# Where the operand sums of one weight pair are made, and when one stage asks for its factors, in an fp32 encoder block

## The chip, the cores and the metric

The kernel runs on one core of a Trainium2 chip, with five engines that work side by side: PE (TensorE, matrix products), DVE (VectorE), ACT (ScalarE), POOL (GpSimd) and SP (SyncE, which here only issues DMAs). Each engine takes its instructions in program order and waits on semaphores for the others. The metric is the device time of one execution in microseconds (us); three runs of the kernel before were timed, and one more was profiled.

## The reference, cut to what matters

One layer over 1024 tokens of width 1024, all in fp32. `w_in` holds the columns of all the projections side by side.

```python
h = rmsnorm(x, norm_g)
q, k, v, za, u, vs, zs, gm = split(h @ w_in)
a = window_sink_attention(rope(q), rope(k), v, sinks)
a = (a * silu(za)) @ w_att_out
sgo = chunked_spatial_gating(gelu(u), gelu(vs), ...)     # 128x128 mixing per channel group
sgo = (sgo * silu(zs)) @ w_sg_out
ga, gs = split(sigmoid(gm + b_merge))
y = ga * a + gs * sgo
out = rmsnorm(x + y @ w_o, final_g)
```

The change lies in the projections zs (its silu multiplies the gated branch) and gs (one of the two merge gates).

## The kernel before, in words

**Products.** The weights are packed as 82 tiles `w[i]` of 128 x 1024. All large products but that of `vs` are made by a Strassen-Winograd scheme on pairs of weight tiles (`gemm_pair`, L364 for the matmuls): a pair has four quarters of 128 x 512, a11 and a12 (the halves of its first tile) and a21 and a22 (of its second), and takes seven products in place of eight. Their left sides are a11, a12, a22 and four sums of quarters: s1 = a21 + a22, s2 = s1 + a11, s3 = a11 + a21, and s4 = a12 + s2, with the signs folded elsewhere. Each product is 12 matmuls: every operand is split into a rounded part (`wh`, an ACT cast, L154) and a rest (`wl`, a DVE subtraction, L155), and high x high, high x low and low x high are added in PSUM over four slices. In time the seven products run in the order 0, 2, 3, 1, 4, 5, 6; products 2 and 3 need the tile with s1 and s2, products 4 and 5 the one with s3 and s4.

**Two ways to the sums.** A pair made with `pair_job` loads its quarters (four DMAs of 256 KB, tiles `wr`) and DVE adds them (`sums`, L251 to L255: four instructions into two `s` tiles). For a pair made with `early_job` the sums are made in DRAM long before, by six DMAs of the POOL queue, some of them with an adding write (L310, tile `sums`); the pair then loads a11 and a12 as one DMA, a22 as another, and the two tiles of sums (`s<-sums`, 2 x 512 KB). These six steps of all such pairs, with 16 steps for `w_o`, stand in a list `early`, sorted so that step 0 of a first group of eight pairs comes first, then step 1 of all eight, and so on, and then the rest. `part_of_early` takes one from the list: in the `vs` stage at every second call and at every call of its fifth tile (`1 if t == 4 else 2`), in the u pairs at each product, and again in the locked stage below. Each waits for the latest `pace` instruction of a product.

**Order of the pairs.** u (4 pairs), kv (1), q (4), zs (2 of its 4), then the locked stage with gs (4) and ga (4), then zs (2), za, and the output projections. A pair's job begins (its loads are issued, and its splits enter a list) when one split of the pair before is left (`split_next`). `make_sums` gives DVE its additions: in a pair of the zs stage right behind the split for product 6 of the pair that runs.

**The zs stage (`zs_pair`).** For each of its four output tiles ACT takes silu (L1079), DVE multiplies by a factor that an earlier stage left in DRAM (L1088), and the product goes to DRAM (L495). The first zs pair loads its factors as two DMAs of 512 KB into `qhl` tiles, which the q stage used until then; the second loads four of 256 KB into `rot` tiles. The program's names for these DRAM tensors drop the digits, so the factors appear as `qhl<-s_dr` and `rot<-s_dr`, all at L201, the helper that issues on SP's queue. Between the zs products `hook()` runs what is left of the q stage: the first query tiles (`q<-q_hl`) and the last rotation.

**The locked stage.** Each of its eight pairs (`locked_pair`) interleaves the seven products with attention for four steps; PE, ACT and DVE follow an order written by hand here. The scores of a step (L1135) go to two PSUM banks `ps_sc`. For the step, DVE takes maxima (L1160) and ACT exponentials (L1170), and only then are the banks free for the next step's scores. In the first locked pair the scores of step 0 stand ahead of product 0, and those of step 1 in the middle of product 2. Banks `ps_o` are two as well: product 2 of a pair takes the one in which product 5 of the pair before ended, once DVE has read that (L406, which ends the pair's third output tile).

Elsewhere the scheduler of the program chooses the order on each engine, from the program's order and its own estimates.

Of the kernel before, what the change touches and what calls it, by code (L numbers as in the profile page):

```python
# [25 lines left out]
F32 = mybir.dt.float32  # L26
# [5 lines left out]
P = 128  # L32
D = 1024
S = 1024
KC = D // P
HALF = 512
# [11 lines left out]
W_SG = 58  # L48
# [5 lines left out]
def hybrid_tile(  # L54
# [25 lines left out]
    def nm(s):  # L80
        count[0] += 1
        return f"{s}_{count[0]}"
# [4 lines left out]
    def mtile(shape, dt, tag, bufs, pool=None):  # L87
        return (pool or main).tile(shape, dt, name=nm(tag), tag=tag, bufs=bufs)

    def scratch(name, shape=(D, S)):  # L90
        return dram.tile(list(shape), F32, name=name)
# [29 lines left out]
    s1_dr = scratch("s1_dr")  # L121
# [78 lines left out]
    def copy_to(dst, src):  # L200
        nc.sync.dma_start(dst, src)  # L201
# [38 lines left out]
    def half_of(half):  # L240
        return slice(half * HALF, (half + 1) * HALF)
# [26 lines left out]
    def pair_job(n, load):  # L268


        def job():
            r0, r1 = raw_tile(), raw_tile()
            for j in range(2):
                load(r0[:, half_of(j)], 0, j)
            for j in range(2):
                load(r1[:, half_of(j)], 1, j)
            sa, sb = sums(r0[:, 0:HALF], r0[:, HALF:D], r1[:, 0:HALF], r1[:, HALF:D])
            return [
                (r0[:], [(n, 0), (n, 1)]),
                (sa, [(n, 2), (n, 3)]),  # L280
                (sb, [(n, 4), (n, 5)]),
                (r1[:, HALF:D], [(n, 6)]),
            ]

        return job
# [5 lines left out]
    early = []  # L291
# [12 lines left out]
    def early_job(n, i0, i1):  # L304

        made = dram.tile([P, 4, HALF], F32, name=f"sums_{n}")
        s1, s3, s2, s4 = (made[:, i, :] for i in range(4))

        def step(dst, src, op=ALU.bypass):
            return lambda: paced(nc.gpsimd.dma_start(dst, src, accum_op=op))  # L310

        early.append(
            (
                step(made[:, 0:2, :], w[i1][:, 0:HALF].unsqueeze(1).broadcast_to([P, 2, HALF])),
                step(made[:, 2:4, :].rearrange("p a n -> p (a n)"), w[i0]),
                step(s1, w[i1][:, HALF:D], ALU.add),
                step(s3, w[i0][:, 0:HALF], ALU.add),
                step(s2, s1, ALU.add),
                step(s4, s2, ALU.add),
            )  # L320
        )

        def job():
            r0, r1 = raw_tile(), raw_tile()
            copy_to(r0[:], w[i0])
            copy_to(r1[:, HALF:D], w[i1][:, HALF:D])
            loaded = []

            def load_sums():
                for a in range(2):  # L330
                    v = mtile([P, D], F32, "s", 2)
                    copy_to(
                        v[:].rearrange("p (b n) -> p b n", b=2),
                        made[:].rearrange("p (b a) n -> p a b n", a=2)[:, a],
                    )
                    loaded.append(v)

            sums_to_load.append(load_sums)
            if not locked[0]:
                load_made()  # L340
            return [
                (r0[:], [(n, 0), (n, 1)]),
                (lambda: loaded[0][:], [(n, 2), (n, 3)]),
                (lambda: loaded[1][:], [(n, 4), (n, 5)]),
                (r1[:, HALF:D], [(n, 6)]),
            ]

        return job
# [66 lines left out]
    def of_w(i0, i1):  # L415
        return lambda dst, i, j: copy_to(dst, w[(i0, i1)[i]][:, half_of(j)])

    def of_token_w(base, m):


        def load(dst, i, j):
            first, c0 = base + 4 * ((m + i) // 4) + 2 * j, ((m + i) % 4) * P
            d = dst.rearrange("p (c k n) -> p c k n", c=2, k=2)
            for c in range(2):
                copy_to(d[:, c], w[first + c].rearrange("p (k n) -> p k n", k=2)[:, :, c0 : c0 + P])

        return load
# [8 lines left out]
    def add_pairs(base, step, pairs, made=False):  # L436
        for m in pairs:
            i0, i1 = base + step * m, base + step * (m + 1)
            if made:
                jobs.append(early_job(len(jobs), i0, i1))  # L440
            else:
                load = of_w(i0, i1) if step else of_token_w(base, m)
                jobs.append(pair_job(len(jobs), load))

    ALL = range(0, KC, 2)
# [1 line left out]
    jobs.append(pair_job(len(jobs), of_kv))  # L447
    add_pairs(W_Q, 0, ALL)
    add_pairs(W_ZS, 1, (0, 2))
    add_pairs(W_SG, 2, ALL, True)  # L450
    add_pairs(W_ATT, 2, ALL, True)
    add_pairs(W_ZS, 1, (4,), True)
    add_pairs(W_ZS, 1, (6,))
# [3 lines left out]
        add_pairs(base, 2, (4, 6))  # L457
    N_PAIRS = len(jobs)
    written[0] = N_PAIRS
    early = [steps[i] for some in (early[:KC], early[KC:]) for i in range(6) for steps in some]  # L460


    def o_quarter(j, half):
# [22 lines left out]
    def part_of_early(every=2):  # L486
        hooks[0] += 1
        if early and hooks[0] % every == 0:
            early.pop(0)()
# [4 lines left out]
    def put(dst, m, half, src, queue=nc.sync):  # L494
        queue.dma_start(place(dst, m, half), src)  # L495

    def get(src, m, half, bufs, tag="g"):
        g = mtile([P, HALF], F32, tag, bufs, pool)
        copy_to(g[:], place(src, m, half))
        return g  # L500
# [99 lines left out]
    def vs_step(acc, t, k, wh, wl):  # L600

        hi, lo = (v[:, k % 4, :] for v in quarter_of(t, k // 4))
        for n, (lt, rt) in enumerate(((hi, wh), (hi, wl), (lo, wh))):
            mm = nc.tensor.matmul(acc, lt, rt, start=k == 0 and n == 0, stop=k == KC - 1 and n == 2)  # L604
        return mm
# [47 lines left out]
    def vs_weights(c):  # L653
        raw = raw_tile()
        nc.sync.dma_start(raw[:], w[W_VS + 4 + c])
        hi = mtile([P, D], F32R, "wh", 3)
        lo = mtile([P, D], F32R, "wl", 3)
        split(hi[:], lo[:], raw[:])
        return hi, lo
# [55 lines left out]
    for c in range(4):  # L715
        if c + 2 < 4:
            weights.append(vs_weights(c + 2))
        for t in range(NT):
            wh, wl = weights[c]
            for k in range(2):  # L720
                ks = half_of(k)
                pace[0] = vs_step(accs[t][:], t, 2 * c + k, wh[:, ks], wl[:, ks])
            part_of_early(1 if t == 4 else 2)
            if c == 3:
                nc.scalar.activation(xh[:, t, HALF:D], accs[t][:], AF.Gelu)
            if aside and t % 2:
                aside.pop(0)()
# [18 lines left out]
    pool = stage.enter_context(tc.tile_pool(name="mixing", bufs=1))  # L746
    late = []

    def hook():
        for _ in range(2):  # L750
            if late:
                late.pop(0)()
# [84 lines left out]
    pool = stage.enter_context(tc.tile_pool(name="keys", bufs=1))  # L837
# [44 lines left out]
    pool = stage.enter_context(tc.tile_pool(name="queries", bufs=1))  # L882
# [141 lines left out]
    steps = [(g, t, par) for g in range(2) for t in range(NT) for par in range(2)]  # L1024
# [47 lines left out]
    gates = []  # L1072
    last_silu = [None]

    def zs_pair(m, hook):
        silus, hooked = [], [0]

        def finish(i, half, q, src, sign):
            last_silu[0] = nc.scalar.activation(q[:], src, AF.Silu, scale=sign)  # L1079
            silus.append((i, half, q))  # L1080

        def step():
            hook()
            hooked[0] += 1
            if hooked[0] >= 4:
                while silus:
                    i, half, q = silus.pop(0)
                    nc.vector.tensor_mul(q[:], q[:], gates.pop(0))  # L1088
                    put(s_dr, m + i, half, q[:])

        if m:
            gates.extend(get(s1_dr, m + i, half, 5, "rot")[:] for i, half in ((0, 0), (1, 1), (0, 1), (1, 0)))
        else:
            rows = [mtile([P, 2, HALF], F32, "qhl", 3, pool) for _ in range(2)]
            for i in range(2):
                copy_to(rows[i][:].rearrange("p h n -> p (h n)"), s1_dr[i * P : (i + 1) * P, :])
            gates.extend(rows[i][:, half, :] for i, half in ((0, 0), (1, 1), (0, 1), (1, 0)))
        gemm_pair(hb, finish, step)

    steps_of_q += [first_loads(), rotate(1, 1)]  # L1100
    zs_pair(0, part_of_q)
    zs_pair(2, part_of_q)
    after(nc.scalar.activation(warm[:], eps_sb[:], AF.Exp), last_silu[0])
    stage.close()
# [3 lines left out]
    pool = stage.enter_context(tc.tile_pool(name="attention", bufs=1))  # L1108
# [304 lines left out]
    with tc.manual_schedule(engines={mybir.EngineType.PE, mybir.EngineType.Activation, mybir.EngineType.DVE}):  # L1413
        p = 0
# [27 lines left out]
    pool = stage.enter_context(tc.tile_pool(name="later", bufs=1))  # L1442
# [248 lines left out]
    rows = [load_rows(p) for p in range(3)]  # L1691
# [9 lines left out]
    for p in range(4):  # L1701
        n, t, acc, x11 = N_PAIRS + p, T_ORDER[p], accs[p], firsts[p]
# [173 lines left out]
```

## Time and profile before

| | us |
|---|---|
| three runs | 935.73, 934.78, 933.14 (median 934.78) |
| profiled execution | 935.56 |
| its span, first to last instruction | 933.8 |
| PE busy | 910.1 |
| DVE busy | 690.6 |
| ACT busy | 530.3 |
| POOL busy | 147.0 |

The span is what the rows of the trace lie in; 1.8 us of the profiled time lie around it. A row of the timeline has the start in us from the span's start, the duration, engine and line, the operation with output and inputs, and in brackets how long the engine had stood idle before it and what ended that. In a row of the windows stand PE, PEld (weight load), DVE, ACT and POOL busy time, then the clock granted to PE (1 is full), the mean busy share of the 16 DMA engines and GB/s.

### The profile page before, as it was taken

What the parts mean: (1) busy time and instruction counts of PE and PEld (TensorE: products, weight loads), DVE (VectorE), ACT (ScalarE), POOL (GpSimd) and SP (SyncE); (2) the same over time, 40 slices, a digit from 0 to 9 for tenths busy, and PEclk for the clock granted to TensorE, in tenths of its full rate; (3) what the DMA queues carried; (4) which work ended last, traced back from release to release, by engine and by line L of the source; (5) the groups of instructions that cost most, each with busy time, mean ns of one, the idle gap of its engine ahead of it and who ended that gap; (6) DMA issues with size and microseconds to landing.
All of it is one profiled execution on the core that took longest, in us unless ns stands there. A gap on an engine that the chain in (4) does not pass through costs nothing.

```text
span 933.8 us, 13145 instructions
## 1 busy us (share of the span) xinstructions
PE 910.1 (97%) x4285; PEld 752.5 (81%) x4285; DVE 690.6 (74%) x1230; ACT 530.3 (57%) x1054; POOL 147.0 (16%) x215
## 2 busy tenths in 40 slices
PE   7999999999999989999999999999999999999996
PEld 5788888888888768888888887888887887888885
DVE  5784686665677747778887788666699689669986
ACT  6873433333444546777777778443475565458443
POOL 1002322213011002212221111101110011210012
PEclk9999999999999999999999999999999999999999
DMA  7239988877788879999999897775558654999623
GB/s 251 99 113 232 222 155 182 176 162 219 239 273 261 257 248 302 249 263 248 252 328 263 237 273 201 266 239 179 180 199 315 211 197 157 294 295 302 208 108 118
DMA packets 129708, 209.50 MB, mean 224 GB/s; under 512 B 12680, under 2 KB 59272, under 8 KB 129640
## 3 DMA queue, kind: packets, MB, share of 16 engines
q1 hardware_dynamic: 107256, 147.58, 49.4%
q0 software_dynamic: 22240, 60.83, 27.3%
q8 instruction: 34, 0.56, 0.2%
q14 instruction: 34, 0.28, 0.1%
q10 hardware_dynamic: 144, 0.26, 0.1%
HBM read 151.87 MB, written 92.41 MB: 262 GB/s over the span
## 4 chain that ended last, share of the span: by engine, by line
PE 39%; DVE 13%; ACT 7%; issue 3%; DMA 1%; ACTq 0%; DVEq 0%
PE ps_mm L364 19%; PE ps_o L364 11%; PE ps_tp L364 3%; ACT pr L1170 2%; PE ps_sc L364 2%; DVE sm L1160 2%; DVE aT L1273 1%; DVE pTb L1242 1%; ACT pr L1193 1%; PE ps_sc L1135 1%; PE ps_o L1259 1%; DVE wl L155 1%; DVE bq L184 1%; ACT aT L1272 1%; DVE pT L1234 1%
## 5 line engine op out<-in xcount | busy, mean ns | idle before, releaser
L154 ACT CAST wh<-s 128x1024 fp32r<-128x1024 f32 (+1 forms) x78 | 78.0, 1002 | 86.1 <-PE ps_mm L364 39.8
L155 DVE TENSOR_TENSOR wl<-s,wh 128x1024 fp32r<-128x1024 f32 (+1 forms) x78 | 91.4, 1172 | 26.0 <-ACT wh L154 25.8
L155 DVE TENSOR_TENSOR wl<-wr,wh 128x1024 fp32r<-128x1024 f32 (+1 forms) x64 | 60.4, 947 | 58.1 <-ACT wh L154 57.8
L154 ACT CAST wh<-wr 128x1024 fp32r<-128x1024 f32 (+1 forms) x64 | 52.9, 829 | 78.0 <-PE ps_mm L364 38.0
L310 POOL DMA_DIRECT2D sums<-in_w_dram x52 | 39.0, 903 | 218.7 <-PE ps_mm L604 64.3
L1170 ACT ACTIVATE pr<-ps_sc,sm 128x192 f32<-128x192 f32 (+2 forms) x128 | 51.2, 407 | 32.7 <-DVE sm L1161 24.6
L364 PE MATMUL ps_o<-T_b22h,wh 128*128 128x512 f32 x148 | 59.3, 401 | 0.0
L364 PE MATMUL ps_o<-T_t1h,wh 128*128 128x512 f32 x148 | 59.1, 399 | 0.3 <-ACT wh L154 0.2
L364 PE MATMUL ps_o<-T_t1h,wl 128*128 128x512 f32 x148 | 58.3, 394 | 0.0
L364 PE MATMUL ps_o<-T_t1l,wh 128*128 128x512 f32 x148 | 58.1, 393 | 0.0
L364 PE MATMUL ps_o<-T_b22h,wl 128*128 128x512 f32 x148 | 57.8, 390 | 0.0
L364 PE MATMUL ps_o<-T_b22l,wh 128*128 128x512 f32 x148 | 57.8, 390 | 0.0
L364 PE MATMUL ps_mm<-T_b11h,wl 128*128 128x512 f32 x140 | 54.8, 392 | 2.1 <-DVE wl L155 2.1
L364 PE MATMUL ps_mm<-T_t2h,wh 128*128 128x512 f32 x140 | 55.5, 396 | 0.8 <-ACT x L385 0.8
L364 PE MATMUL ps_mm<-T_b11h,wh 128*128 128x512 f32 x140 | 55.1, 393 | 0.0
L364 PE MATMUL ps_mm<-T_t4h,wh 128*128 128x512 f32 x140 | 54.9, 392 | 0.0
L364 PE MATMUL ps_mm<-T_t3h,wh 128*128 128x512 f32 x140 | 54.8, 391 | 0.0
L364 PE MATMUL ps_mm<-T_b11l,wh 128*128 128x512 f32 x140 | 54.7, 391 | 0.0
L364 PE MATMUL ps_mm<-T_t3h,wl 128*128 128x512 f32 x140 | 54.6, 390 | 0.0
L364 PE MATMUL ps_mm<-T_t4h,wl 128*128 128x512 f32 x140 | 54.6, 390 | 0.0
L364 PE MATMUL ps_mm<-T_t2h,wl 128*128 128x512 f32 x140 | 54.6, 390 | 0.0
L364 PE MATMUL ps_mm<-T_t2l,wh 128*128 128x512 f32 x140 | 54.6, 390 | 0.0
(370 smaller groups left out, 2474.3 us busy)
## 6 DMA issues: line engine op xcount, KB each, us to landing
wr<-in_w_dram SPq DMA_DIRECT2D x77, 256.0 KB
sums<-in_w_dram POOLq DMA_DIRECT2D x26, 512.0 KB, 8.2
s<-sums SPq DMA_DIRECT2D x26, 512.0 KB
wr<-in_w_dram SPq DMA_DIRECT2D x17, 512.0 KB
q_hl<-qhl SPq DMA_DIRECT2D x16, 512.0 KB
q<-q_hl SPq DMA_DIRECT2D x64, 128.0 KB
y_dr<-x POOLq DMA_DIRECT2D x28, 256.0 KB, 6.4
sums<-in_w_dram POOLq DMA_DIRECT2D x26, 256.0 KB, 8.1
```

The costliest lines, as they stand in the source:

```text
L154: nc.scalar.copy(hi, src)
L155: return nc.vector.tensor_sub(lo, src, hi.bitcast(F32))
L184: op(dst[:, i : i + 2, :], a[:, i : i + 2, :], c[:, i : i + 2, :])
L310: return lambda: paced(nc.gpsimd.dma_start(dst, src, accum_op=op))
L364: nc.tensor.matmul(acc, lt, rt, start=fresh and k == 0 and n == 0, stop=k == 3 and n == 2, skip_group_check=True,)
L1135: nc.tensor.matmul(sc[:, i, lo:hi], q_of[:, c, i * P : (i + 1) * P], kt[:, f, lo:hi], start=f == 0, stop=f == 1,)
L1160: nc.vector.tensor_reduce(st.nmax[:, c, :], st.sc[c][:, :, lo:hi], axis=mybir.AxisListType.X, op=ALU.min)
L1170: nc.scalar.activation(st.pr[:, i, place_of(c, lo, hi)], st.sc[c][:, i, lo:hi], AF.Exp, bias=st.nmax[:, c, i : i + 1], scale=-1.0, accum_o ...
L1193: nc.scalar.mul(v, v, st.inv[:, c, i : i + 1])
L1234: nc.vector.tensor_sub(st.a[:, 1, :], st.inner[:], st.a[:, 0, :].bitcast(F32))
L1242: nc.vector.tensor_sub(st.b[lo, cols(c)], st.ends[hi, 0:256], st.b[hi, cols(c)].bitcast(F32))
L1259: nc.tensor.matmul(st.po[:, cs], lt, rt, start=i == 0, stop=i == len(terms) - 1, skip_group_check=True)
```

## The change

```diff
     add_pairs(W_ZS, 1, (0, 2))
-    add_pairs(W_SG, 2, ALL, True)
+    add_pairs(W_SG, 2, (0,))
+    add_pairs(W_SG, 2, (2, 4, 6), True)
...
-    early = [steps[i] for some in (early[:KC], early[KC:]) for i in range(6) for steps in some]
+    early = [steps[i] for some in (early[: KC - 1], early[KC - 1 :]) for i in range(6) for steps in some]
...
-            part_of_early(1 if t == 4 else 2)
+            part_of_early()
...
         def step():
             hook()
             hooked[0] += 1
+            if m == 0 and hooked[0] == 1:
+                rows = [mtile([P, 2, HALF], F32, "qhl", 3, pool) for _ in range(2)]
+                for i in range(2):
+                    copy_to(rows[i][:].rearrange("p h n -> p (h n)"), s1_dr[i * P : (i + 1) * P, :])
+                gates.extend(rows[i][:, half, :] for i, half in ((0, 0), (1, 1), (0, 1), (1, 0)))
...
         if m:
             gates.extend(get(s1_dr, m + i, half, 5, "rot")[:] for i, half in ((0, 0), (1, 1), (0, 1), (1, 0)))
-        else:
-            rows = [mtile([P, 2, HALF], F32, "qhl", 3, pool) for _ in range(2)]
-            for i in range(2):
-                copy_to(rows[i][:].rearrange("p h n -> p (h n)"), s1_dr[i * P : (i + 1) * P, :])
-            gates.extend(rows[i][:, half, :] for i, half in ((0, 0), (1, 1), (0, 1), (1, 0)))
```

The first gs pair becomes a `pair_job`: four loads of 256 KB in place of one of 512 KB, one of 256 KB and two of 512 KB, four additions on DVE, and six steps fewer in `early` (88 in place of 94; the first group has seven pairs, and the `vs` stage takes 16 steps in place of 20). The factors of the first zs pair are asked for after that pair's first product, behind the first query tiles on SP's queue.

The orders of the built program show what the scheduler makes of it. PE and ACT keep their order to the instruction. DVE gets its four additions around the second zs pair's first output tile, right behind the split for product 6 of that pair; and in that pair two of the four multiplications by factors move from behind the split of s1 and s2 to ahead of L406, the addition that ends the third output tile. In the first zs pair the first multiplication moves behind the addition L402, and the second behind the split of the next sums. On SP's queue the two `s<-sums` loads of the first gs pair are gone, so that the four `rot` factors follow directly on one `s_dr` write, and the `qhl` factors stand behind the six query loads. POOL has five rows of DMAs fewer, and the DMA that it issues in the second zs pair keeps its form.

## Prediction

> **What bounds the kernel now.** First the page and the list of PE's waits, then windows of 3.41 us around the longest wait (and, last, around a shorter one), to see the clock.
>
> ```profile
> PE 910.1 (97%) x4285; PEld 752.5 (81%) x4285; DVE 690.6 (74%) x1230; ACT 530.3 (57%) x1054; POOL 147.0 (16%) x215
> ...
> PE ps_sc L1135 <- ACT pr L1170: 4.3, 1, 4.3
> PE ps_mm L364 <- DVE wl L155: 2.1, 2, 1.1
> ...
> 343.05:346.46 3.41, 1.22 (x5) 0.67 (x4) 3.18 (x5) 2.16 (x4) 0.00 (x0) 1.00 0.68 261
> 346.46:349.87 3.41, 1.32 (x6) 1.32 (x7) 2.19 (x9) 1.57 (x10) 0.00 (x0) 0.50 0.82 234
> 349.87:353.29 3.42, 3.42 (x12) 2.64 (x12) 1.39 (x7) 1.69 (x7) 1.38 (x2) 0.50 1.02 331
> 790.20:793.60 3.40, 2.29 (x10) 1.80 (x10) 3.40 (x6) 0.00 (x0) 0.87 (x1) 1.00 0.31 99
> ```
>
> PE is busy for 97% of the span, so a change elsewhere counts only where PE stands still. One place is worth most: a wait of 4.3 us for the score banks, at the start of the locked stage. Behind it PE is granted half its clock for two windows, in which it works 1.32 + 3.42 = 4.74 us; at full clock that is 2.37 us, so 2.37 us are lost beside the wait. The place costs 4.28 + 2.37 = 6.65 us. Everything that the change moves ends just ahead of it.
>
> Next the timelines of PE, ACT, DVE, SP and POOL there (SPq is SP's issue of a DMA, not its transfer).
>
> ```profile
> 342.61 0.39 PE L364 MATMUL ps_o<-T_t1h,wh 128*128 128x512 f32 x1
> 343.87 0.40 PE L364 MATMUL ps_o<-T_t1h,wl 128*128 128x512 f32 x1
> 348.55 1.97 PE L1135 MATMUL ps_sc<-k,q 128*128 128x64 f32 x8 [4.28 <-ACT pr L1170]
> ...
> 340.71 1.05 ACT L154 CAST wh<-s 128x1024 fp32r<-128x1024 f32 x1 [5.70 <-DMA s<-sums]
> 341.67 0.62 ACT L1079 ACTIVATE x<-x 128x512 f32<-128x512 f32 x1
> 342.20 1.04 ACT L154 CAST wh<-s 128x1024 fp32r<-128x1024 f32 x1
> 349.79 0.69 ACT L1193 ACTIVATE pr<-pr,sm 128x128 f32<-128x128 f32 x2 [0.50 <-DVE sm L1185]
> ...
> 328.69 0.69 DVE L155 TENSOR_TENSOR wl<-wr,wh 128x512 fp32r<-128x512 f32 x1 [0.72 <-ACT wh L154]
> 330.94 0.69 DVE L397 TENSOR_TENSOR x<-x,ps_o 128x512 f32<-128x512 f32 x1 [1.56 <-PE ps_o L364]
> 331.80 1.23 DVE L155 TENSOR_TENSOR wl<-wr,wh 128x1024 fp32r<-128x1024 f32 x1 [0.17 <-DMA q_hl<-qhl]
> 336.38 0.69 DVE L406 TENSOR_TENSOR x<-x,ps_o 128x512 f32<-128x512 f32 x1 [2.03 <-PE ps_o L364]
> 341.79 1.23 DVE L155 TENSOR_TENSOR wl<-s,wh 128x1024 fp32r<-128x1024 f32 x1 [4.72 <-ACT wh L154]
> 343.23 2.10 DVE L1088 TENSOR_TENSOR x<-x,rot 128x512 f32<-128x512 f32 x3 [0.21 <-DMA rot<-s_dr]
> 345.24 1.22 DVE L155 TENSOR_TENSOR wl<-s,wh 128x1024 fp32r<-128x1024 f32 x1
> 346.38 0.68 DVE L1088 TENSOR_TENSOR x<-x,rot 128x512 f32<-128x512 f32 x1
> 347.15 0.29 DVE L1160 TENSOR_REDUCE sm<-ps_sc 128x2 f32<-128x128 f32 x1
> ...
> 320.47 0.88 SPq L201 DMA_DIRECT2D wr<-in_w_dram  x2
> 324.74 5.14 SPq L919 DMA_DIRECT2D q_hl<-qhl  x8
> 329.93 1.65 SPq L201 DMA_DIRECT2D s<-sums  x2
> 331.63 0.59 SPq L495 DMA_DIRECT2D s_dr<-x  x1
> 332.26 4.59 SPq L201 DMA_DIRECT2D rot<-s_dr  x4
> ...
> 329.44 0.72 POOL L310 DMA_DIRECT2D sums<-in_w_dram  x1 [43.68 <-ACT x L392]
> ```
>
> Read from the end: PE waits until 348.55 for ACT's exponentials, these for DVE's maxima (347.15, 1.40 us ahead of PE's resumption), and the maxima stand on DVE behind the last factor multiplication (346.38) and the split of s3 and s4 (345.24). Those are late for two transfers: ACT idles 5.70 us until the sums land at 340.7, though they were asked for at 329.93, and the first `rot` factor is there only at 343.2, though asked for at 332.26. DVE has 4.72 us of idle time just before. The bound here is what arrives, not what computes.
>
> **The change, part by part.**
>
> *Sums on DVE.* Four additions (about 0.69 us each, starting some 0.60 apart) are added behind 329.3, where DVE idles 1.56 us up to L397. The other 0.9 us push L397 and the split at 331.80 by 0.3 to 0.5 us; DVE then idles until 336.38 and again until 341.79, and product 0, the first to need that split, starts at about 339.6 (342.61 less twelve matmuls of 0.25, the mean pitch from 342.61 to 343.87). On the path: nothing. Should that cover go, the price would be those 0.9 us.
>
> ```profile
> L254 DVE TENSOR_TENSOR s<-wr x20: 684/690/693, 94.7 to 821.4; 128x512 f32<-128x512 f32 x20
> ...
>   DMA wr<-in_w_dram: 24.0, 9
> ...
> 340.00:342.00 2.00, 2.00 (x10) 1.61 (x10) 0.21 (x1) 1.29 (x2) 0.00 (x0) 1.00 1.05 406
> ...
> sums<-in_w_dram POOLq DMA_DIRECT2D x1, 512.0 KB, 9.4
> sums<-in_w_dram POOLq DMA_DIRECT2D x26, 512.0 KB, 8.2
> sums<-in_w_dram POOLq DMA_DIRECT2D x1, 512.0 KB, 5.0
> ...
> 382.08 0.53 POOL L310 DMA_DIRECT2D sums<-in_w_dram  x1 [14.86 <-ACT x L1331]
> 380.00:400.00 20.00, 20.00 (x106) 16.70 (x106) 15.96 (x41) 16.24 (x49) 6.86 (x9) 1.00 0.96 226
> ```
>
> *Loads.* Four issues of 0.44 us in place of two at 320.47 keep SP 0.9 us longer, but the next issue there waits until 324.74 anyway. The quarters have from 322.2 to 329.3 to land. They are 0.26 MB more; the two `s<-sums` (1.05 MB, 1.65 us of issue) go.
>
> *What is late next: the factors.* ACT no longer waits for a DMA, and its cast of s1 and s2 moves ahead of 338. But two multiplications now stand ahead of L406 on DVE, and L406 (whose bank product 2 needs at 342.61) ahead of the splits. Let g be the time at which the second factor is there. From the spacing of the rows: multiplication 0.67, L406 0.69, ACT's silu and, 0.53 behind its start, the second cast 1.04 (up to g + 3.0); DVE meanwhile splits s1 and s2 (1.22) and makes the third multiplication; then the split of s3 and s4 (1.14 to the next), the last multiplication and 0.77 to the maxima: they start at g + 5.0, and PE resumes at g + 6.4. PE reaches this point at 344.27, so the stall is **g - 337.9 us**, and none below that.
>
> Both ends for g. Before, the first factor landed at 343.2, and the second 0.65 us later if 0.26 MB move at the 406 GB/s of 340 to 342: 343.9. Take out 1.05 MB of sums ahead of it at that rate, 2.6 us: **341.3**. That leaves POOL's 512 KB transfer from 329.44 as long as it was, 9.4 us. The median of its kind is 8.2, and one issued at 382.08, in a stretch as full (share 0.96), took 5.0 (in the rows above: this transfer's own, the median, and the one at 382.08); here it shared the engines with the eight `q_hl` writes and the sums, of which the sums go. With 5.0 it would be gone at 334.4, and s_dr and two factors (0.79 MB, 1.9 us) could land at **336.3**, early enough for no stall. I take 7.5 us, between these but nearer the median: 1.9 us less, g = 339.4. The stall is 1.5 us, and 4.28 - 1.5 = 2.8 us are saved.
>
> *The clock.* A window with PE busy for 1.22 us of 3.41 was followed by half clock, one with 1.32 kept it there, one with 2.29 did no harm. So the limit lies at an idle time between 1.1 and 2.1 us in one window; I take the middle, 1.6. A stall of 1.5 stays just under it, and the 2.37 us are saved too. This is the weakest step.
>
> The Trainium skill, "TensorE: Matmul & The Clock Gate", section "What's actually happening", has the half rate return after at least one idle window of about 3.4 us, free-running. By that rule no stall under 3.4 us would cost the clock. The trace differs: the window ahead of the drop was not idle, it held 1.22 us of work; the measurement decides.
>
> *Behind the stall.* PE then makes the scores (1.97 us at half clock, so about 1.0) and the second half of product 2 (six matmuls of 0.25), from 345.8 to 348.3; the transposes after it need the weighing that ended at 349.79 + 0.69, 3.3 us behind the maxima, now 347.7. So no new wait of note.
>
> *Factors of the first zs pair.*
>
> ```profile
> 307.64 1.12 SPq L201 DMA_DIRECT2D qhl<-s_dr  x2
> 308.81 4.03 SPq L1058 DMA_DIRECT2D q<-q_hl  x6
> ...
> 314.85 0.68 DVE L1088 TENSOR_TENSOR x<-x,qhl 128x512 f32<-128x512 f32 x1
> ```
>
> They are issued some 4 us later, behind six query loads; their first user moves from 314.85 to about 316.1, behind L402. If they land late, DVE idles, with L406 and the rotation behind it; 0.72 + 1.56 us of idle time up to L397 take that up. Between nothing and 1 us; I take nothing. The query tiles are first needed for the scores ahead of product 0, about 338.6, so their earlier issue gains nothing.
>
> *POOL.* Six DMAs fewer, of which none stands in PE's waits: nothing. POOL's order of DMAs keeps one of the same form at 329.44.
>
> **Sum.** 2.8 + 2.4 = 5.2 us off the profiled 935.56 (span 933.8 and 1.8 around it): **930.4 us**. The median of three, 934.78, is 0.8 lower than the profiled run, which may have had a longer stall than most; the range takes that in.
>
> **The rivals.**
>
> *The stall only shrinks, and the clock still halves.* With g at 340.4 the stall is 2.5 us, over the limit wherever the window falls: 1.8 us saved, **933.8**. For it: the DMA engines' share is 0.68 to 1.05 in the windows shown, and the limit is known only to a microsecond. Against it: the sums were the larger half of what stood ahead of the factors.
>
> *POOL's transfer keeps its 9.4 us.* It is not moved, and the factors take the sums' place beside it. Then g = 341.3, the stall 3.4, the clock halves: 0.9 us saved, **934.7**. For it: 9.4 us was measured in this place; against it, no other in the rows shown took so long. The Trainium skill, "DMA: Bandwidth & Descriptors", section "Queues, rings and completion order", says that each DMA engine takes turns between the queues with work; by that rule the factors would share with POOL just as the sums did. The 9.4 us against 8.2 and 5.0 agree that transfers slow each other.
>
> *Slower: the factors hold L406.* Before, L406 ran at 336.38 whatever the factors did; now it waits for two. From g = 342.15 on, the maxima come later than 347.15, and each further us costs one. If the factors land no earlier than now, at 343.9, PE also stands from 342.61 on for the bank, and the end is 1.8 us later: **937.3**. Against it: 1 MB less stands ahead of them. The quarters landing late (DVE waited 24.0 us in nine such places, row above) would do the same through L254, which precedes L397; seven us of lead speak against that.
>
> **How the numbers follow.** Forecast 0.47 (930.4; by itself 928.5, the whole 6.65 saved and a little more, to 931.9); the shrunk stall 0.31 (933.8, of which 0.04 under 932.0); POOL's length 0.13 (934.7); slower 0.09 (937.3, of which 0.04 over 937.6). The range 928.5 to 935.4 leaves out 0.09 + 0.05 above and 0.04 below. A measurement of this kernel can tell about 0.3% from no change, 2.8 us: faster (under 932.0) 0.47 + 0.04 = 0.51, slower 0.04, the same 0.45.
>
> **What would show it.** In the profile after: no ACT wait on `s<-sums` near 340; DVE's two factor multiplications, now after L402, waiting for `rot<-s_dr` until about 339; PE's wait for `ps_sc` at 1.5 us; a granted clock of 1.00 at 346 to 353. Wrong it is if that wait stays over 2 us with 0.50 behind it, if PE waits for `ps_o` near 342.6, or if DVE waits for `wr` at 329.

## The result and the profile after

| | before | after |
|---|---|---|
| median of seven runs, us | 934.78 (933.13 to 936.38) | 930.57 (928.11 to 931.29) |
| profiled execution, us | 935.56 | 928.11 |
| its span, us | 933.8 | 926.3 |

The ratio is 0.9951, with a 95% interval of 0.9935 to 0.9968: 0.5% faster. The forecast was 930.4. The profiled execution is the fastest of the seven after: its mean granted clock is 0.999, as in the one at 928.47, and 0.995 or 0.996 in the five others, which so ran longer at half clock, at places that no profile shows.

In the profile after, the windows around the wait for `ps_sc`, cut where the clock's own windows lie:

```profile
340.44:343.85 3.41, 2.88 (x16) 2.15 (x16) 2.19 (x9) 2.30 (x12) 0.00 (x0) 1.00 0.79 209
343.85:347.27 3.42, 3.42 (x20) 2.83 (x20) 2.13 (x9) 3.13 (x14) 1.38 (x2) 1.00 1.07 322
```

The granted clock stays at 1.00 where it was 0.50. Now the timelines of PE, ACT, DVE and SP, and the row of POOL's transfer in the list of DMA issues (its last column is the time from issue to landing):

```profile
340.49 0.39 PE L364 MATMUL ps_o<-T_t1h,wh 128*128 128x512 f32 x1
342.50 1.39 PE L1136 MATMUL ps_sc<-k,q 128*128 128x64 f32 x8 [0.49 <-ACT pr L1171]
345.16 0.60 PE L1207 MATMUL ps_tp<-ident,pr 128*64 128x128 f32 x4
...
334.09 1.05 ACT L154 CAST wh<-s 128x1024 fp32r<-128x1024 f32 x1 [1.19 <-PE ps_o L364]
...
327.18 0.68 DVE L254 TENSOR_TENSOR s<-wr 128x512 f32<-128x512 f32 x1
331.54 0.69 DVE L402 TENSOR_TENSOR x<-x,ps_mm 128x512 f32<-128x512 f32 x1
335.60 1.35 DVE L1094 TENSOR_TENSOR x<-x,rot 128x512 f32<-128x512 f32 x2 [3.37 <-DMA rot<-s_dr]
336.86 0.68 DVE L406 TENSOR_TENSOR x<-x,ps_o 128x512 f32<-128x512 f32 x1
341.10 0.29 DVE L1161 TENSOR_REDUCE sm<-ps_sc 128x2 f32<-128x128 f32 x1
...
318.95 1.86 SPq L201 DMA_DIRECT2D wr<-in_w_dram  x4
322.79 5.63 SPq L920 DMA_DIRECT2D q_hl<-qhl  x8
329.03 3.32 SPq L201 DMA_DIRECT2D rot<-s_dr  x4
```

```profile
sums<-in_w_dram POOLq DMA_DIRECT2D x1, 512.0 KB, 6.6
```

ACT casts s1 and s2 at 334.09 and waits for no DMA. DVE's four additions begin at 327.18 without a wait. What DVE waits for now are the factors (3.37 us), with L406 behind them. All four quarter loads stand ahead of the eight `q_hl` writes on SP.

**Where the time came from.** One more row of PE's timeline of before gives the place where the two programs are level again:

```profile
352.99 0.75 PE L1206 MATMUL ps_tp<-ident,pr 128*64 128x128 f32 x4
```

| stretch of PE | before | after | saved |
|---|---|---|---|
| up to product 2 of the first locked pair | 342.61 | 340.49 | 2.12 |
| its first half, up to the wait | 1.66 | 1.52 | 0.14 |
| wait for ps_sc | 4.28 | 0.49 | 3.79 |
| scores and second half, up to the transposes | 4.44 | 2.66 | 1.78 |

The place itself gave 0.14 + 3.79 + 1.78 = 5.71 us. The 2.12 us ahead of it are not shown to be the change's. Near the program's start the two executions differ in their clock, as the windows show, first of before and then of after:

```profile
8.54:11.95 3.41, 1.29 (x6) 0.72 (x5) 2.48 (x3) 3.41 (x7) 2.37 (x1) 1.00 1.03 420
11.95:15.37 3.42, 3.42 (x10) 2.64 (x9) 3.01 (x9) 2.86 (x5) 0.00 (x0) 0.50 0.79 300
```

```profile
9.33:12.74 3.41, 1.95 (x7) 1.42 (x8) 2.93 (x5) 3.29 (x7) 1.91 (x1) 1.00 1.03 419
12.74:16.16 3.42, 3.34 (x17) 2.21 (x16) 3.28 (x8) 3.28 (x5) 0.00 (x0) 1.00 0.55 203
```

A window in which PE works at half clock throughout costs 3.42 / 2 = 1.7 us at most. PE's instructions there are the same in both programs; the windows' boundaries fall 0.8 us apart. Behind it the same matmul starts at 19.89 before and at 18.59 after, so 1.3 us of the lead come from there. Most of the rest comes at 306.12, where PE waits 0.80 us for ACT's copy (L385) before and not at all after. Shortly ahead of that ACT waited for a write of query tiles (`q_hl<-qhl`), 2.85 us before and 1.89 after. This wait doesn't follow the edits: e4 below, with neither of them, has none, and e2, with one, has 0.32 us. So some 2 of the 7.45 us between the two profiled executions may well be chance, and the medians (4.2 us apart) are the better measure.

### The profile page after: what moved, and what is told of

Read it like the earlier page. It is cut to its first block, busy times and chain, and to the rows that moved or that the text cites. A ratio compares the mean times of both kernels' runs of the same rounds, so it can differ in the third digit from the quotient of the medians.

```text
span 926.3 us, 13136 instructions
## 1 busy us (share of the span) xinstructions
PE 907.4 (98%) x4285; PEld 749.9 (81%) x4285; DVE 691.7 (75%) x1234; ACT 530.8 (57%) x1054; POOL 141.1 (15%) x209
## 4 chain that ended last, share of the span: by engine, by line
PE 34%; DVE 14%; ACT 7%; issue 4%; DMA 3%; SPq 0%; ACTq 0%; DVEq 0%
PE ps_mm L364 17%; PE ps_o L364 10%; PE ps_tp L364 2%; ACT pr L1171 2%; PE ps_sc L364 2%; DVE sm L1161 2%; DVE pTb L1243 1%; DVE aT L1274 1%; ACT pr L1194 1%; DVE wl L155 1%; DVE bq L184 1%; PE ps_o L1260 1%; PE ps_sc L1136 1%; ACT aT L1273 1%; DMA s<-sums 1%
## 5 line engine op out<-in xcount | busy, mean ns | idle before, releaser
L364 PE MATMUL ps_mm<-T_t4l,wh 128*128 128x512 f32 x140 | 54.5, 390 | 0.0
```

What stands on the lines that cost most here:

```text
L364: nc.tensor.matmul(acc, lt, rt, start=fresh and k == 0 and n == 0, stop=k == 3 and n == 2, skip_group_check=True,)
```

## The experiments

The theory that the experiments set out from is that of the prediction, with the gain put down to the sums: the two `s<-sums` loads no longer stand ahead of the factors. The rival puts it down to the other edit. Line numbers shift by a few where a kernel has lines of its own. Ratios are to the kernel before on the same chip, with the 95% interval.

### Each edit alone

**e1_sums_only**: the changed kernel with the factors of the first zs pair asked for where they were.

```diff
-            if m == 0 and hooked[0] == 1:
-                rows = [...]; copy_to(...); gates.extend(...)
...
+        else:
+            rows = [...]; copy_to(...); gates.extend(...)
```

> The changed kernel with the factors of the first zs pair asked for at their old place. Theory (the gain comes from the two loads of sums that no longer stand ahead of the second zs pair's factors): PE's wait for the score banks stays under 1.5 us and the time is within 1 us of the changed kernel, about 930.5 us. Rival (the gain comes from the later request of the factors, which lets the query tiles go first): back to about 934.8 us, with a wait of about 4 us for the score banks.

Measured: 935.0 us, ratio 1.0001 (0.9985 to 1.0016). No gain. SP, DVE and PE:

```profile
321.03 1.35 SPq L201 DMA_DIRECT2D wr<-in_w_dram  x3
324.88 5.86 SPq L920 DMA_DIRECT2D q_hl<-qhl  x8
330.79 0.63 SPq L201 DMA_DIRECT2D wr<-in_w_dram  x1
...
338.84 0.69 DVE L254 TENSOR_TENSOR s<-wr 128x512 f32<-128x512 f32 x1 [4.51 <-DMA wr<-in_w_dram]
...
344.33 0.51 PE L364 MATMUL ps_o<-T_t1h,wl 128*128 128x512 f32 x1 [1.13 <-DVE wl L155]
347.92 1.33 PE L1136 MATMUL ps_sc<-k,q 128*128 128x64 f32 x5 [2.38 <-ACT pr L1171]
```

The scheduler's order has only three of the four quarter loads ahead of the eight writes. The fourth is issued at 330.79, and the additions start at 338.84 instead of some 329. PE stands for 1.13 and 2.38 us, and the clock halves behind it. The time is the rival's, but the rows show a late quarter and not query tiles that come too late; e5 below decides between them.

**e2_factors_only**: the kernel before, with only the factors of the first zs pair moved.

```diff
+            if m == 0 and hooked[0] == 1:
+                rows = [...]; copy_to(...); gates.extend(...)
...
-        else:
-            rows = [...]; copy_to(...); gates.extend(...)
```

> The kernel before with only the factors of the first zs pair asked for a product later. Theory: nothing is gained, 934.8 us within 1 us, and PE still waits about 4 us for the score banks, behind factors that land at about 343. Rival (the move of the request carries the gain): about 931 us.

Measured: 929.24 us, ratio 0.9948 (0.9930 to 0.9966). The whole gain, against the theory. SP and ACT:

```profile
320.44 0.57 SPq L201 DMA_DIRECT2D s<-sums  x1
323.27 5.73 SPq L919 DMA_DIRECT2D q_hl<-qhl  x8
...
334.56 1.05 ACT L154 CAST wh<-s 128x1024 fp32r<-128x1024 f32 x1 [1.19 <-DMA q_hl<-qhl]
```

Here the scheduler put the load of s1 and s2 ahead of the writes, and ACT casts them at 334.56; PE's wait for `ps_sc` is 0.68 us and the clock stays full. So the theory as put, that the sums alone bring the gain, fell. Both kernels point at one thing: what stands behind the eight writes on SP's queue. That became the next theory.

### The order on SP's queue held apart from the edits

**e5_sums_quarters_first**: e1, with the writes of the last rotation handed to SP at a later point of the program, so that all four quarter loads come first.

```diff
-        for at, dst in places:
-            nc.sync.dma_start(dst, hl[at].bitcast(F32))
+        late_writes.extend((dst, hl[at].bitcast(F32)) for at, dst in places)
+        if not to_hold[0]:
+            write_late()
...
+            to_hold[0] = True
             hook()
             hooked[0] += 1
+            if (m, hooked[0]) == (0, 7):
+                write_late()
```

> The sums on DVE, the factors of the first zs pair at their old place, and the eight q_hl writes of the last rotation given to SP late enough that all four quarter loads of the gs pair stand ahead of them, as in the changed kernel; DVE's and SP's orders then differ from the changed kernel's in nothing but the place of the two qhl factor loads and of their first multiplication. Theory (the sums bring the gain, and the second edit matters only because it puts the fourth quarter ahead of the writes): 930.5, 0.45% under the kernel before; no wait of DVE at the first addition (L254), a wait for ps_sc under 1.2 us, the clock full behind it. Rival (the place of the factors itself carries the gain): within 0.15% of the kernel before, 935, with a wait for ps_sc over 2 us and the half clock.

Measured: 930.62 us, ratio 0.9943 (0.9926 to 0.9959). The theory held. SP, DVE and PE:

```profile
321.42 1.82 SPq L201 DMA_DIRECT2D wr<-in_w_dram  x4
...
329.61 0.68 DVE L254 TENSOR_TENSOR s<-wr 128x512 f32<-128x512 f32 x1
...
345.23 1.39 PE L1147 MATMUL ps_sc<-k,q 128*128 128x64 f32 x8 [0.80 <-ACT pr L1182]
```

The additions wait for nothing, and the wait for `ps_sc` is 0.80 us. The old place of the factors costs nothing that can be measured.

**e6_factors_writes_first**: e2, with both loads of sums held behind the last of the writes, and the `rot` factors behind the sums.

```diff
+                    if last_write:
+                        after(load, last_write.pop())
+                    last_sums[:] = [load]
...
+        if tag == "rot" and last_sums:
+            after(load, last_sums[0])
```

> The kernel before with the factors of the first zs pair asked for later and nothing else, and SP's order held to the one of before in the second zs pair: both loads of sums behind the q_hl writes, and the rot factors behind these. Theory (the factors' place alone brought the full gain only because the scheduler then put one of the two loads of sums ahead of the writes): within 0.15% of the kernel before, 935, with ACT waiting some 5 us for the sums, a wait for ps_sc of about 4 us and the half clock behind it. Rival (fewer transfers in the way early, or SP being done sooner): 929 to 931, and a wait for ps_sc under 1.2 us.

Measured: 935.45 us, ratio 0.9994 (0.9983 to 1.0005). The theory held: the gain is gone. SP, now with the sums behind the writes, ACT and PE, and then the window that holds the wait and the next:

```profile
330.26 1.22 SPq L334 DMA_DIRECT2D s<-sums  x2
...
338.14 1.05 ACT L154 CAST wh<-s 128x1024 fp32r<-128x1024 f32 x1 [3.68 <-DMA s<-sums]
...
346.02 1.88 PE L1142 MATMUL ps_sc<-k,q 128*128 128x64 f32 x8 [2.43 <-ACT pr L1177]
```

```profile
342.76:346.18 3.42, 0.99 (x6) 0.53 (x4) 2.88 (x8) 0.92 (x6) 0.00 (x0) 1.00 0.93 323
346.18:349.59 3.41, 3.41 (x13) 3.02 (x14) 1.79 (x9) 2.34 (x12) 0.88 (x2) 0.50 0.92 274
```

The wait of 2.43 us is shorter than the 4 us expected, but it brings the half clock all the same.

### POOL's transfer

**e3_after_pool_later** and **e4_before_pool_later**: the changed kernel and the kernel before, with POOL's 512 KB DMA of the second zs pair taken from its list two places later.

```diff
-            part_of_early(1 if p < 5 else 2)
+            if (p, at) != (0, 0):
+                part_of_early(1 if p < 5 else 2)
+            if (p, at) == (0, 3):
+                part_of_early(1)
```

> The changed kernel, with the one 512 KB DMA of POOL that runs in the second zs pair given two places later (first step of the locked stage skipped, two steps at its third product). Theory (POOL's transfer shares the DMA engines with the factors and still sets their landing): DVE's wait for the second factor, 3.4 us in the changed kernel, shrinks by 1 to 3 us, PE's wait for the score banks goes to 0; the time falls by 0.5 us at most where that wait was 0.5, by up to 3 us in runs where the clock still dropped. Rival (the transfer does not matter, the factors wait for the eight writes of the rotated queries): DVE's wait stays at 3 us or more, and the time is unchanged.

> The kernel before, with the same DMA of POOL given two places later. Theory: sums and factors land 1.3 us (512 KB at 406 GB/s) to 4 us earlier, PE's wait for the score banks falls from 4.3 us to between 0.5 and 3 us: 931 to 933.5 us. Rival (it is the bytes of the sums alone, or the DVE order): 934.8 us within 1 us.

Measured: 927.83 us, ratio 0.9934 (0.9914 to 0.9954), and 928.4 us, ratio 0.9933 (0.9918 to 0.9947). In e3 DVE's wait for the factors fell from 3.37 to 1.49 us. SP and ACT in e4:

```profile
327.73 1.68 SPq L201 DMA_DIRECT2D s<-sums  x2
...
334.17 1.05 ACT L154 CAST wh<-s 128x1024 fp32r<-128x1024 f32 x1 [1.39 <-PE ps_o L364]
```

With the transfer away, the sums of the kernel before land in time although they stand behind the writes, and neither kernel has a wait for `ps_sc`. For e4 that is more than expected: a wait of 0.5 to 3 us was to be left. The kernel before needs no change of sums at all, then: of its transfers from 324 on it is enough to move one away. The Trainium skill, "DMA: Bandwidth & Descriptors", section "Queues, rings and completion order", lets each DMA engine take turns between the queues with work. What e4 shows fits that: ACT's cast of s1 and s2 waits 1.39 us for PE, where before it waited 5.70 us for the sums. The turns themselves no row shows.

**e7_keep_steps**: the changed kernel, with POOL's six DMAs for the first gs pair left in; nobody reads what they write.

```diff
+    early_job(len(jobs), W_SG, W_SG + 2)
     add_pairs(W_SG, 2, (0,))
...
-    early = [... early[: KC - 1], early[KC - 1 :] ...]
+    early = [... early[:KC], early[KC:] ...]
...
-            part_of_early()
+            part_of_early(1 if t == 4 else 2)
```

> The changed kernel, with POOL's six DMAs for the sums of the first gs pair left in the list and issued as before, although nobody reads what they write. Theory (POOL's six DMAs are worth nothing, as the prediction had it): the changed kernel's 930.6 within 0.15%, a wait for ps_sc under 1.2 us. Rival (the six DMAs fewer, and what they took from the other transfers, are a part of the gain): 0.15% or more above the changed kernel, 932 and over, with a transfer that lands late.

Measured: 929.77 us, ratio 0.9939 (0.9923 to 0.9955): the six DMAs are worth nothing. DVE, PE and two windows:

```profile
337.58 1.34 DVE L1095 TENSOR_TENSOR x<-x,rot 128x512 f32<-128x512 f32 x2 [4.71 <-DMA rot<-s_dr]
...
344.49 1.39 PE L1137 MATMUL ps_sc<-k,q 128*128 128x64 f32 x8 [1.84 <-ACT pr L1172]
```

```profile
340.38:343.79 3.41, 2.27 (x10) 1.52 (x9) 3.29 (x7) 2.79 (x5) 0.00 (x0) 1.00 0.65 215
343.79:347.21 3.42, 2.68 (x15) 2.24 (x16) 2.22 (x12) 2.92 (x15) 0.02 (x1) 1.00 0.84 238
```

In this execution the factors were late and the wait was 1.84 us, which the expectation had under 1.2. A boundary cut it into 1.1 and 0.7 us, and the clock stayed up.

### The clock's limit

**e8_maxima4** and **e9_maxima7**: the changed kernel with one small DVE step made over, to lengthen the wait.

```diff
-            of(maxima, a, 0)
+            for _ in range(1 if p else 4):     # e9: 7
+                of(maxima, a, 0)
```

> The changed kernel, with DVE's maxima of the first half of step 0 made four times over in the first locked pair, 0.40 us each (341.10 to 341.50 in the profile of the changed kernel), so that the wait for ps_sc grows by 1.2 us, from 0.5 to 1.7. Theory (the clock falls when PE idles between 1.50 and 1.66 us of one window of 3.41 us, as the windows of the runs so far bear out: 1.91 us of work kept it full, 1.75 did not): most of this wait in one window is just over the limit, the clock halves for two windows at this place in the runs in which the boundary does not split the wait; between 1.2 us (split) and 4.6 us (not split, up to 3.4 us more) over the changed kernel, 931.8 to 935. Rival (the limit lies at 2.1 us idle or over, nearer to the 1.21 us of work seen in the kernel before): 1.2 us over the changed kernel, 931.8, and the clock full.

> The same with the maxima made seven times over: 2.4 us more, a wait for ps_sc of 2.9 us. Both theories: the clock halves for two windows unless a boundary splits the wait into pieces under the limit; 2.4 us of wait and up to 3.4 us of clock over the changed kernel, 933 to 936, about the kernel before. A full clock with a wait of 2.9 us in one window, and 933.0, would speak against any limit under it.

Measured: 933.67 us, ratio 0.9978 (0.9966 to 0.9990), and 935.1 us, ratio 0.9999 (0.9991 to 1.0008): 3.1 and 4.5 us over the changed kernel's 930.57. One repetition took 0.52 us, not 0.40 (e8's maxima start at 342.88 and 343.40 in the rows of DVE), so the doses were 1.6 and 3.1 us. Windows of e8, the first two at the place, the last two near the start:

```profile
342.35:345.77 3.42, 0.66 (x3) 0.19 (x2) 2.90 (x12) 1.25 (x7) 0.00 (x0) 1.00 0.70 198
345.77:349.18 3.41, 3.34 (x12) 3.06 (x13) 1.86 (x9) 2.57 (x13) 0.65 (x1) 0.50 1.04 329
...
7.85:11.26 3.41, 1.77 (x9) 1.03 (x9) 2.31 (x4) 3.38 (x5) 2.24 (x1) 1.00 1.03 420
11.26:14.67 3.41, 3.22 (x8) 2.55 (x9) 3.00 (x8) 3.21 (x7) 0.13 (x1) 0.50 0.98 382
```

```profile
342.88 0.29 DVE L1161 TENSOR_REDUCE sm<-ps_sc 128x2 f32<-128x128 f32 x1
343.40 0.29 DVE L1161 TENSOR_REDUCE sm<-ps_sc 128x2 f32<-128x128 f32 x1
```

An added wait of 1.6 us brought 3.1 us; the rest, 1.5 us, is near the 1.78 us that full clock gave behind the wait in the table above, so the half clock is its likely cause. e9's profiled wait is 5.1 us, against 2.9 expected, with half clock for two windows behind it. But e8's profiled wait came out at 2.8 us, in one window, so the dose missed the stretch between the two theories, and by itself it doesn't tell them apart. The start of the program does: the same idle spells are cut there at another point in each execution. PE's work of 1.77 us in a window was followed by half clock, and in a profile of the changed kernel taken once more (e11 below) 1.90 us by full clock:

```profile
9.32:12.73 3.41, 1.90 (x7) 1.34 (x8) 2.98 (x5) 3.22 (x7) 1.96 (x1) 1.00 1.03 422
12.73:16.15 3.42, 3.37 (x18) 2.23 (x17) 3.28 (x8) 3.28 (x5) 0.00 (x0) 1.00 0.58 215
```

So the limit lies between 1.5 and 1.64 us of idle time in one window, for the matmuls that run there. One window speaks against a single figure: in the last products of the changed kernel 1.62 us of work (917.31 to 920.73) was followed by a window still at full clock, in which PE had nothing to do, while near the start of e9 1.62 us of work (7.55 to 10.96) was followed by half clock. What the chip counts there stays open.

### The order on DVE, and the best version

**e10_factors_behind**: the changed kernel, with the two multiplications that had gone ahead of L406 held behind the split of s1 and s2, as before.

```diff
-            if hooked[0] >= 4:
+            if hooked[0] >= (6 if m else 4):
...
-                    nc.vector.tensor_mul(q[:], q[:], gates.pop(0))
+                    by_factor = nc.vector.tensor_mul(q[:], q[:], gates.pop(0))
+                    if m:
+                        after(by_factor, last_split[0])
```

> The changed kernel, with the two multiplications by factors that went ahead of L406 held behind the split of s1 and s2 on DVE, as in the kernel before. Theory (what the changed kernel loses by DVE's wait of 3.37 us ahead of L406 is at most the 0.5 us of its wait for ps_sc): within 0.15% of the changed kernel, 930 to 930.6, DVE's split of s1 and s2 2 us earlier, the maxima 0.5 to 1 us earlier and no wait for ps_sc. Rival (the order costs or brings more, through the bank that L406 holds or the transfers behind the multiplications): over 1 us from the changed kernel, either way.

Measured: 928.35 us, ratio 0.9927 (0.9913 to 0.9940), 2.2 us under the changed kernel's median where at most 0.5 was expected. The two ratios' intervals overlap (the changed kernel has 0.9935 to 0.9968), so the size of this gain is not certain. DVE:

```profile
334.72 0.69 DVE L407 TENSOR_TENSOR x<-x,ps_o 128x512 f32<-128x512 f32 x1 [2.03 <-PE ps_o L365]
335.63 1.22 DVE L155 TENSOR_TENSOR wl<-s,wh 128x1024 fp32r<-128x1024 f32 x1 [0.23 <-ACT wh L154]
337.21 2.10 DVE L1095 TENSOR_TENSOR x<-x,rot 128x512 f32<-128x512 f32 x3 [0.36 <-DMA rot<-s_dr]
341.14 0.29 DVE L1164 TENSOR_REDUCE sm<-ps_sc 128x2 f32<-128x128 f32 x1
```

The factors came 1.6 us later than in the profile of the changed kernel (337.21 against 335.60), yet the maxima start at the same time, 341.1, and PE doesn't wait: DVE used the time up to the factors for L407 and the split. The expectation took the 0.49 us of one profile for the usual wait, which may be why it was too low. In the other profiles with the new order on DVE and all quarters ahead of the writes it was 0.80 (e5), 1.84 (e7) and 1.26 (e11, below).

**e11_after_again** is the changed kernel once more; **e12_factors_behind_pool_later** has the edits of e10 and of e3 together.

> The changed kernel itself, timed beside the next one. Theory (its stall ahead of the scores differs from run to run with the landing of the factors, 0.5 us in its profile, but 0.8 in that of sums_quarters_first and 1.8 in that of keep_steps, the same order there but for the qhl factors and POOL's DMAs; where it passes the clock's limit the half clock comes on top): 930.5 within 0.15%, with single runs from 928 to 932. Rival (the differences seen between the kernels so far are those of their chips and sessions): as low as the kernel with the factors behind, 928.4.

> The changed kernel with both reliefs: the two multiplications held behind the split of s1 and s2, and POOL's 512 KB transfer taken two places later. Theory (each of them alone takes the stall away in nearly every run, 928.4 and 927.8, so both together have nothing left to take): 927.5 to 928.5, no wait for ps_sc, no run at 931. Rival (POOL's transfer costs more than this stall, and the order more than this stall, so that they add): 926.5 or less.

Measured: 929.11 us, ratio 0.9944 (0.9926 to 0.9962), and 927.56 us, ratio 0.9919 (0.9904 to 0.9933). DVE and PE in e11:

```profile
336.90 0.69 DVE L1094 TENSOR_TENSOR x<-x,rot 128x512 f32<-128x512 f32 x1 [0.35 <-DMA rot<-s_dr]
341.75 0.29 DVE L1161 TENSOR_REDUCE sm<-ps_sc 128x2 f32<-128x128 f32 x1
...
343.15 1.39 PE L1136 MATMUL ps_sc<-k,q 128*128 128x64 f32 x8 [1.26 <-ACT pr L1171]
```

e11 is the changed kernel on another chip, and its 929.11 lies at the low edge of the theory's 930.5 within 0.15%, with runs from 927.42 to 934.15, wider than forecast. So the rival is not ruled out: a part of the 2.2 us between e10 and the changed kernel can be the chips'. e12 is the fastest by its median, 7.2 us under the kernel before and 1.6 under the changed kernel beside it (the intervals of those two still overlap, from 0.9926 to 0.9933). It adds little to e10 or e3 alone, as the theory has it: once the wait is gone, there is nothing more at this place.

## Why the prediction was right

**The bound.** Right. PE's wait for `ps_sc` and the half clock behind it were worth 5.71 us of the 6.65 in the profiles. The runs sort by it: in the five profiles with a wait of 2.38 us or more there (before, e1, e6, e8, e9) the clock halves for two windows behind it and the medians are 933.7 to 935.5 us; in the nine others the wait is 1.84 us or less, the clock stays full and the medians are at most 930.6.

**The sum.** Its total fits better than its terms, and that is partly luck. It takes 5.2 us off a profiled run that was 0.8 above its median; the medians are 4.2 apart, the profiled executions 7.45.

**Sums on DVE: nothing.** Right. The additions start at 327.18 without a wait, and L402 ends at 332.2 with 3.37 us of idle time behind it.

**Loads: the quarters land in time.** Right for this program, but it hangs on more than the prediction said. It read SP's order from the program with both edits in it. With the sums alone (e1), one of the four loads falls behind the writes and all is lost; the 935.0 came by the mechanism that the prediction named under its slower rival, quarters that land late through L254, though no slower than before.

**What is late next.** Right in its chain. From the start of the second factor's multiplication, at g, the maxima were put at g + 5.0 and PE at g + 6.4; e11 has 341.75 - 336.90 = 4.85 and 343.15 - 336.90 = 6.25. The rule for the stall, g - 337.9, holds too: in the profile after, the second multiplication starts at 335.60 + 0.67 = 336.27, which is 338.39 with the 2.12 us by which PE is ahead there, and the wait is 0.49. The stall was put at 1.5 us, from g = 339.4; four profiles have 0.49, 0.80, 1.26 and 1.84. The one shown here is the shortest, so its 3.8 us saved, against 2.8, is partly chance.

**POOL's transfer at 7.5 us.** The value is within what was seen, the reason is not borne out. It took 6.6 us after, and 6.4 in e6 with both sums still beside it, where before it took 9.4; and 8.1 in e7, without the sums. These are the rows, of e6 and then of e7:

```profile
sums<-in_w_dram POOLq DMA_DIRECT2D x1, 512.0 KB, 6.4
```

```profile
sums<-in_w_dram POOLq DMA_DIRECT2D x1, 512.0 KB, 8.1
```

Its length differs between executions more than by what the change takes away. That it stands there at all is what matters (e3, e4).

**The clock.** Right, and close: the limit was taken at 1.6 us of idle time in a window, and the runs have it between 1.5 and 1.64, with the reservation above. What the full clock saves was mis-sized: put at 2.37 us, it was 1.78, in the main because the scores took 1.39 us at full clock (the row at 342.50) where half of 1.97 was reckoned with. And a stall of 2.5 us need not be over the limit "wherever the window falls", as the prediction had it: cut in its middle it would be 1.25 and 1.25, under the limit, as the 1.84 us of e7 were cut. The Trainium skill, "TensorE: Matmul & The Clock Gate", section "What's actually happening", lets the half rate return after an idle window. By that rule e6 would have kept its clock; its window held 0.99 us of work and was followed by 0.50. That the windows run free of the program, as the Trainium skill has it there, the runs bear out: near the start their boundaries lie at 8.54 us in the profile before and at 9.33 after.

**Factors of the first zs pair: nothing.** Right as a cost: with all quarters first, e5 has them at the old place and 0.9943, the changed kernel at the new one 0.9951 and 0.9944. But "nothing" hid their effect. Through the scheduler they decide which loads stand ahead of the eight writes, and without them the first edit brings nothing (e1), while by themselves they bring all (e2). The prediction asked what the moved loads cost and whom they delay, and not what the program would be without them; the number didn't need that, the credit does.

**POOL's six DMAs fewer: nothing.** Right (e7).

**The slower rival, that the factors hold L406.** It didn't come to a slower kernel, but its mechanism is there in small: L406 at 336.86 stands behind a wait of 3.37 us, and in the order that avoids this (e10) PE doesn't wait even with factors that land 1.6 us later. By the medians it is 2.2 us faster, with the doubt named above.

## What to carry to other kernels

Before crediting a change of data flow, look at which loads with a due time stand behind a block of writes on the same issuing engine; here the place of one 256 KB or 512 KB load among eight writes decided over 4 us, and edits that seemed unrelated moved it. Where several transfers pile up ahead of one wait, any one taken away may bring the whole gain, and the second little (e2, e4 and e12 here), so test each edit alone and with the order held. An engine that must wait for a late transfer should do first what doesn't need it.

## What the runs showed of the hardware

The clock's windows run free of the program, so that the same idle spells cost a half clock in one execution and not in the next: at the start of the program 1.29 us of work in a window was followed by half clock in the profile before, 1.95 by full clock in the profile after, from the same instructions. That put the second execution 1.3 us ahead there. And a wait that a boundary cuts in two (1.84 us in e7) costs only itself, while a wait of 2.43 us that lies in one window (e6) cost two windows at half clock besides (346.2 to 353.0).
